# Two up pairs of seven products follow each other, and a down group's first splits stand behind mixer work

## The chip, the cores and the metric

The kernel runs on one core of a Trainium2 chip. The metric is the device time of one execution in microseconds (us), taken as the median of several runs. Engines are named as in the profile: PE (TensorE, matmuls), PEld (TensorE's weight loads), DVE (VectorE), ACT (ScalarE), POOL (GpSimd), SP (SyncE, which only issues transfers).

## The reference, cut to what matters

A trunk of four layers on x of 512 tokens by 1024 channels, all float32. Each layer has a token mixer (convolution, attention on a 64-wide grid, retention, convolution) and then a gated feed-forward part, which is what the change touches:

```
def conv_ffn(h, w_up, dw_w, dw_b, w_down):
    u = dwconv(h @ w_up, dw_w, dw_b)          # 1024 -> 5632 channels, 3 taps over the tokens
    val, gate = jnp.split(u, 2, axis=-1)      # 2816 each
    return (jax.nn.gelu(gate) * val) @ w_down # 2816 -> 1024
...
    h = rmsnorm(x, norm2_g[i])
    x = x + conv_ffn(h, ffn_w_up[i], ffn_dw_w[i], ffn_dw_b[i], ffn_w_down[i])
```

## The kernel before, in words

Channels lie on the 128 partitions and the 512 tokens along the free dimension. A float32 product is made of three passes: each operand is split into a high part (rounded to the matmul's format, a cast on ACT) and a low part (the rest, a subtraction on DVE), and `mm3` (lines 180 to 183) adds high times high, low times high and high times low. So every weight tile that comes in by a transfer costs one ACT cast (line 167) and one DVE subtraction (line 168) in `split_w`. Some up tiles are made in another way (`load_w_acc`, lines 171 to 178): ACT makes both parts and an accumulating transfer on POOL completes the low one.

The feed-forward part (`ffn`, line 298) has 22 pairs j of up tiles, n = 2j (value) and n = 2j + 1 (gate), each of 128 channels by 512 tokens. `ups_of(j)` (line 599) makes pair j, `mids(j)` (line 588) runs the mixer steps up to pair j - 1: the three taps (lines 403 to 407), gelu (411), the product of value and gate (426). Two mixed pairs make one unit H of four quarters and three sums of quarters (lines 426 to 432), which is split into Hh and Hl (line 435, by `split`, lines 191 and 192).

Two places use seven products in place of eight (a 2 by 2 scheme in the manner of Strassen) on matmuls of 256 columns. In the up part, four pairs per layer are made so by `up_macro` (line 373); which ones is in `UPS` (line 78). Its last two products are not made in it but in `finish_up` (line 366), which is called after the next up tile, or inside the next `up_macro`; only then is the sum `s12` (line 371) there for the mixer. In the down part, `down` (line 509) takes four H units as a group and makes four output pairs i = 0 to 3; group 0 starts at pair 8 (in layer 1 at pair 9), group 1 at pair 16 (`starts`, line 612). The first products of i = 0 need only the first three H units of the group, the rest the fourth one too.

The weights for seven products come from `sums` (line 466), transfers only: two loads on SP and one accumulating transfer on POOL into the buffers `ws` (three of them) and `wq` (one), and from `weights` (line 478): one raw load on SP, then six DVE operations and four ACT casts into the buffers wh and wl (three each), h2, l2, h4 and l4 (one each). Raw loads go through two buffers `wr` (line 157). `fetch_sums` (line 595) calls `sums` one pair ahead.

The instructions are not executed in the order of the Python text: a scheduler lays out each engine's queue at compile time. It goes through a simulated time and gives an engine that is free the ready instruction that comes first in the program. So the order of the calls is a priority, and the queues are fixed once they are laid out.

Around the start of a group the text of before is, at lines 613 to 619:

```
for j in range(1, FT):
    ups_of(j)
    w0 = down_w(0, starts[j], state["load"]) if j in starts else None
    if n > S2[l]:
        mids(j)
    if w0:
        down(starts[j], w0, lambda: mids(j + 1), lambda: ups_of(j + 1))
```

Here `down_w` (line 496) is `sums` and `weights` together, so the first weights of a group come before the mixer step of the pair that was made last but one. With `UPS` = (10, 12, 18, 19), and (11, 13, 18, 19) in layer 1, one ordinary pair stands between the first two pairs of seven, and none between the last two.

Of the kernel before, what the change touches and what calls it, by code (L numbers as in the profile page):

```python
# [17 lines left out]
P = 128  # L18
# [56 lines left out]
NT_FFN = 7  # L75
NWS = 3
SCALED = (5, 7, 5, 5)
UPS = ((10, 12, 18, 19), (11, 13, 18, 19), (10, 12, 18, 19), (10, 12, 18, 19))
COMBO = (4, 5, 6, 7)
ACC = tuple(n for n in range(3, 2 * FT, 2) if n // 2 not in (8, 9, 16, 17))  # L80


# [1 line left out]
def tile_trunk(  # L84
# [17 lines left out]
    def nm(s):  # L102
        uid[0] += 1
        return f"{s}{uid[0]}"
# [51 lines left out]
    def load_raw(src, n):  # L156
        raw = wraw.tile([P, D], F32, tag="wr", name=nm("wr"))
        state["load"] = nc.sync.dma_start(raw[:, :n], src)
        return raw
# [4 lines left out]
    def split_w(raw, n, eng):  # L164
        hi = whi.tile([P, D], F32R, tag="wh", name=nm("wh"))
        lo = wlo.tile([P, D], F32R, tag="wl", name=nm("wl"))
        nc.scalar.copy(hi[:, :n], raw[:, :n])  # L167
        eng.tensor_tensor(lo[:, :n], raw[:, :n], hi[:, :n].bitcast(F32), SUB)  # L168
        return hi, lo
# [20 lines left out]
    def split(src, hi, lo, n=None):  # L190
        state["cast"] = nc.scalar.copy(hi, src)  # L191
        return nc.vector.tensor_tensor(lo, src, hi.bitcast(F32), SUB)  # L192
# [38 lines left out]
    state = {"late": [], "squares": []}  # L231
# [66 lines left out]
    def ffn(l, after):  # L298
        with ExitStack() as st:
# [37 lines left out]
            def combos(p):  # L337
                e, o = x[2 * p], x[2 * p + 1]
                c = hp.tile([P, D], F32, tag="ws", name=nm("cx"), bufs=NWS)
                q = [c[:, i * 256:(i + 1) * 256] for i in range(4)]  # L340
                nc.vector.tensor_tensor(q[0], e[:, 256:], e[:, :256], SUB)
                nc.vector.tensor_tensor(q[1], o[:, :256], e[:, :256], SUB)
                nc.vector.scalar_tensor_tensor(q[2], o[:, :256], -1.0, q[0], MUL, SUB)
                nc.vector.scalar_tensor_tensor(q[3], q[2], -1.0, o[:, 256:], MUL, SUB)
                cl[p] = hp.tile([P, D], F32R, tag=f"cl{p}", name=nm("cl"))
                for k, h in ((2 * p, slice(0, T)), (2 * p + 1, slice(T, D))):
                    ch[k] = const.tile([P, T], F32R, tag=f"x{k}", name=nm("ch"))
                    split(c[:, h], ch[k], cl[p][:, h])
# [117 lines left out]
            def sums(src, gate=None):  # L466
                n = src.shape[-1] // 4
                r13 = hp.tile([P, D], F32, tag="ws", name=nm("ws"), bufs=NWS)
                sg = hp.tile([P, D], F32, tag="wq", name=nm("wq"))
                with tc.issue_after(gate.ins) if gate else ExitStack():  # L470
                    nc.sync.dma_start(
                        r13[:, :2 * n].rearrange("p (b n) -> p b n", b=2),
                        src[:, 2 * n:3 * n].unsqueeze(1).broadcast_to([P, 2, n]))
                    nc.gpsimd.dma_start(r13[:, :2 * n], src[:, :2 * n], accum_op=ADD)
                    nc.sync.dma_start(sg[:, n:2 * n], src[:, 3 * n:])
                return src, r13, sg

            def weights(src, r13, sg):
                n = src.shape[-1] // 4
                r1 = load_raw(src[:, :2 * n], 2 * n)  # L480
                w1 = split_w(r1, 2 * n, nc.vector)
                w13 = split_w(r13, 2 * n, nc.vector)
                r2 = r13[:, n:2 * n]
                nc.vector.tensor_tensor(r2, r2, r1[:, :n], ADD)
                h2 = hp.tile([P, T], F32R, tag="h2", name=nm("h2"))
                l2 = hp.tile([P, T], F32R, tag="l2", name=nm("l2"))
                split(r2, h2[:, :n], l2[:, :n])
                nc.vector.tensor_tensor(sg[:, :n], r2, sg[:, n:2 * n], ADD)
                h4 = hp.tile([P, D], F32R, tag="h4", name=nm("h4"))
                l4 = hp.tile([P, D], F32R, tag="l4", name=nm("l4"))  # L490
                split(sg[:, :2 * n], h4[:, :2 * n], l4[:, :2 * n])
                u = lambda w, b: (w[0][:, b * n:(b + 1) * n], w[1][:, b * n:(b + 1) * n])
                return {"a11": u(w1, 0), "a22": u(w1, 1), "s3": u(w13, 0), "s1": u(w13, 1),
                        "s2": u((h2, l2), 0), "sg": u((h4, l4), 0), "a12": u((h4, l4), 1)}

            def down_w(i, q, gate=None):
                p0, p1 = PARTS[q]
                c = PART_COL[q]
                return weights(*sums(f_down[l, i][:, c:c + 4 * (p1 - p0) * P], gate))

            def prod(o, w, q, b, start, stop=True, part=None):
                p0, p1 = PARTS[q]
# [6 lines left out]
            def down(q, first, late, filler):  # L509
                p0, p1 = PARTS[q]  # L510

                def finish(i, w, v, s12):
                    prod(v[:, :256], w["sg"], q, 2, False)
                    prod(v[:, 256:], w["a12"], q, 3, True)
                    nc.vector.tensor_tensor(s12, v, s12, ADD)
                    nc.gpsimd.dma_start(xd[2 * i + 1], s12, accum_op=ADD)

                prev = None
                for i in range(4):
                    w = down_w(i, q) if i else first  # L520
                    xb, v = bank(psa), bank(psa)
                    xc = xb[:, :256]
                    s12 = t512()
                    if i == 0:
                        prod(xc, w["a11"], q, 1, True, part=range(p0, p1 - 1))
                        prod(v[:, 256:], w["a22"], q, 6, True, part=range(p0, p1 - 1))
                    now = range(p1 - 1, p1) if i == 0 else None
                    prod(xc, w["a11"], q, 1, True, part=now)
                    nc.scalar.copy(s12[:, 256:], xc)  # L529
                    prod(v[:, 256:], w["a22"], q, 6, True, part=now)  # L530
                    prod(xc, w["s2"], q, 0, False)
                    nc.scalar.copy(s12[:, :256], xc)
                    prod(v[:, :256], w["s1"], q, 4, True)
                    prod(xc, w["s3"], q, 5, False)
                    u2 = t512()
                    nc.scalar.activation(u2.rearrange("p (h t) -> p h t", h=2),
                                         xc.unsqueeze(1).broadcast_to([P, 2, 256]), AF.Copy, scale=-1.0)
                    nc.vector.tensor_tensor(u2, u2, v, SUB)
                    nc.gpsimd.dma_start(xd[2 * i], u2, accum_op=ADD)
                    if prev:  # L540
                        finish(*prev)
                    prev = (i, w, v, s12)
                late()
                filler()
                finish(*prev)
# [42 lines left out]
            def mids(upto):  # L588
                nonlocal done
                while done < upto:  # L590
                    for _ in mid(done, ups[2 * done], ups[2 * done + 1]):
                        pass
                    done += 1

            def fetch_sums(j):
                if j in UPS[l] and j not in ahead:
                    ahead[j] = sums(f_us[l, UPS[l].index(j)], state["load"])

            def ups_of(j):
                nonlocal n  # L600
                fetch_sums(j + 1)
                if j in UPS[l] and n < 2 * j + 2:
                    ups.extend(up_macro(j))
                    n += 2
                while n < 2 * j + 2:
                    ups.append(up(n))
                    finish_up()
                    n += 1
                if j in COMBO:
                    combos(COMBO.index(j))  # L610

            starts = {2 * p1 + (l == 1 and q == 0): q for q, (_, p1) in enumerate(PARTS)}
            for j in range(1, FT):
                ups_of(j)
                w0 = down_w(0, starts[j], state["load"]) if j in starts else None
                if n > S2[l]:
                    mids(j)
                if w0:
                    down(starts[j], w0, lambda: mids(j + 1), lambda: ups_of(j + 1))
            mids(FT)  # L620
# [684 lines left out]
    kind, l = seq[0]  # L1305
    first = []
# [50 lines left out]
def _layout(inp):  # L1357
# [56 lines left out]
    for sh in range(PH):  # L1414
        for r in range(PH):
# [14 lines left out]
        [fu[l, :, par, :, j + c].transpose(1, 0, 2).reshape(P, T)  # L1430
         for c, par in ((0, 0), (FT, 1), (FT, 0), (0, 1))], -1) for j in UPS[l]]) for l in range(DEPTH)])
    fd = f["ffn_w_down"].reshape(4, FT, P, 8, P)
# [50 lines left out]
```

## Time and profile before

| | |
|---|---|
| median of three runs | 2579.05 us (2576.54 to 2581.14) |
| the profiled execution | 2579.95 us |
| its span, from the first to the last instruction | 2577.9 us |
| granted TensorE clock, mean over the span | 0.993 |

Two lines of the page show how work is spread over the span in 40 equal slices, and how many transfers go with it. Each digit is the busy share of a slice in tenths.

```
PE   9999999999999999899999999999999999999999
DVE  7976867677877776667666565686767887686765
ACT  5555645465556554455332323454545445554543
DMA  6736766743333566574222222567565672477664
```

A row of the groups, the timeline or the waits gives line, engine, operation and the names of the tiles, output before input (wl<-wr,wh is the subtraction that makes a low part). Idle time ahead of an instruction stands in brackets in the timeline, with what ended it. The four feed-forward parts lie in the trace at about 190 to 560 us, 800 to 1190, 1620 to 1990 and 2190 to 2578.

### The profile page before, as it was taken

To read this page: it belongs to the slowest core of one execution; us is meant where nothing else is said; L and a number is where in the kernel's file an instruction comes from. 1 tells how busy PE (TensorE), PEld (TensorE's weight loads), DVE (VectorE), ACT (ScalarE), POOL (GpSimd) and SP (SyncE) were. 2 spreads that over 40 slices of the span, in tenths; PEclk is the share of its full clock that TensorE was granted. 3 is DMA by queue.
4 is the path that set the end of the run, shared out by engine and by line. 5 is a ranking of instruction groups with operands and counts; after the bars stand their busy time and mean duration, and the time that the engine had idled before them with its cause. 6 is when DMAs were issued, how large, how long until landed. Compare 5 with 4: busy or idle time off the path is not lost.

```text
span 2577.9 us, 38787 instructions
## 1 busy us (share of the span) xinstructions
PE 2528.4 (98%) x15166; PEld 2182.9 (85%) x15166; DVE 1826.8 (71%) x3004; ACT 1265.2 (49%) x1763; POOL 387.2 (15%) x476
## 2 busy tenths in 40 slices
PE   9999999999999999899999999999999999999999
PEld 7878897989998888798888888789888888789897
DVE  7976867677877776667666565686767887686765
ACT  5555645465556554455332323454545445554543
POOL 1214010104321211020000000201010121101010
PEclk9999999999999999999999999999999999999999
DMA  6736766743333566574222222567565672477664
GB/s 239 233 100 185 196 156 164 161 142 95 97 91 106 141 179 153 148 185 122 82 75 73 82 77 70 146 170 182 153 151 143 202 228 89 119 190 168 166 152 139
DMA packets 124040, 370.70 MB, mean 144 GB/s; under 512 B 15136, under 2 KB 18080, under 8 KB 123856
## 3 DMA queue, kind: packets, MB, share of 16 engines
q1 hardware_dynamic: 90816, 277.30, 34.2%
q0 software_dynamic: 31744, 88.19, 18.4%
q10 hardware_dynamic: 1296, 2.72, 0.3%
q8 instruction: 119, 1.95, 0.3%
q14 instruction: 65, 0.53, 0.1%
HBM read 333.59 MB, written 30.79 MB: 141 GB/s over the span
## 4 chain that ended last, share of the span: by engine, by line
PE 86%; DVE 6%; DMA 4%; ACT 2%; issue 1%; DVEq 0%; POOL 0%; SPq 0%; ACTq 0%; POOLq 0%
PE ps L182 21%; PE ps L183 21%; PE ps L181 21%; PE ps L316 3%; PE ps L312 3%; PE ps L311 3%; PE ps L187 3%; PE ps L188 3%; PE ps L186 3%; DMA wr<-in_f_down 2%; DVE wl L168 1%; PE ps L743 1%; PE ps L742 1%; PE ps L741 1%; PE ps L454 1%
## 5 line engine op out<-in xcount | busy, mean ns | idle before, releaser
L167 ACT CAST wh<-wr 128x1024 fp32r<-128x1024 f32 (+1 forms) x310 | 317.9, 1027 | 567.9 <-PE ps L182 275.3
L168 DVE TENSOR_TENSOR wl<-wr,wh 128x1024 fp32r<-128x1024 f32 (+1 forms) x307 | 371.0, 1208 | 207.9 <-ACT wh L167 192.5
L182 PE MATMUL ps<-xl,wh 128*128 128x512 f32 (+1 forms) x1248 | 488.2, 391 | 0.0
L181 PE MATMUL ps<-xh,wh 128*128 128x512 f32 (+1 forms) x1248 | 485.9, 390 | 1.4 <-ACT wh L167 1.4
L183 PE MATMUL ps<-xh,wl 128*128 128x512 f32 (+1 forms) x1248 | 484.9, 390 | 0.1
L181 PEld LDWEIGHTS ps<-xh,wh 128*128 128x128 f32 x1248 | 235.1, 188 | 55.3 <-ACT wh L167 2.2
L183 PEld LDWEIGHTS ps<-xh,wl 128*128 128x128 f32 x1248 | 234.8, 188 | 52.6 <-DVE wl L168 0.7
L182 PEld LDWEIGHTS ps<-xl,wh 128*128 128x128 f32 x1248 | 235.1, 188 | 51.9 <-DVE xl L253 0.5
L182 PE MATMUL ps<-Hl,wh 128*128 128x256 f32 (+1 forms) x734 | 228.1, 314 | 6.2 <-DVE Hl L192 6.2
L183 PE MATMUL ps<-Hh,wl 128*128 128x256 f32 (+1 forms) x734 | 225.5, 315 | 7.9 <-DVE wl L168 7.6
L181 PE MATMUL ps<-Hh,wh 128*128 128x256 f32 (+1 forms) x734 | 222.4, 315 | 9.3 <-ACT Hh L191 6.3
L311 PE MATMUL ps<-xh,wh 128*128 128x512 f32 x416 | 164.8, 396 | 1.3 <-ACT wh L175 1.3
L312 PE MATMUL ps<-xl,wh 128*128 128x512 f32 x416 | 164.5, 395 | 0.0
L187 PE MATMUL ps<-wl,xh 128*128 128x256 f32 (+1 forms) x512 | 159.2, 312 | 1.9 <-DVE wl L168 1.9
L186 PE MATMUL ps<-wh,xh 128*128 128x256 f32 (+1 forms) x512 | 159.2, 314 | 1.1 <-ACT xh L250 1.1
L188 PE MATMUL ps<-wh,xl 128*128 128x256 f32 (+1 forms) x512 | 159.3, 312 | 0.0
L181 PEld LDWEIGHTS ps<-Hh,wh 128*128 128x128 f32 x734 | 140.7, 194 | 21.3 <-ACT Hh L191 7.4
L183 PEld LDWEIGHTS ps<-Hh,wl 128*128 128x128 f32 x734 | 142.0, 196 | 17.5 <-DVE wl L168 10.5
L182 PEld LDWEIGHTS ps<-Hl,wh 128*128 128x128 f32 x734 | 142.7, 195 | 15.3 <-DVE Hl L192 7.8
L177 POOL DMA_DIRECT2D wl<-in_f_up x52 | 46.7, 897 | 451.1 <-ACT wl L176 401.9
L316 PE MATMUL ps<-xh,wl 128*128 128x512 f32 x416 | 107.8, 400 | 3.3 <-DMA wl<-in_f_up 3.3
L181 PE MATMUL ps<-Hh,h 128*128 128x256 f32 x384 | 108.9, 284 | 0.5 <-ACT t L529 0.5
(330 smaller groups left out, 6167.9 us busy)
## 6 DMA issues: line engine op xcount, KB each, us to landing
wr<-in_f_up SPq DMA_DIRECT2D x144, 512.0 KB, 4.1
wraw<-in_cdw SPq DMA_DIRECT2D x56, 608.0 KB, 5.2
wl<-in_f_up POOLq DMA_DIRECT2D x52, 512.0 KB, 7.8
ws<-in_f_down SPq DMA_DIRECT2D x32, 512.0 KB, 8.5
wr<-in_f_down SPq DMA_DIRECT2D x32, 512.0 KB, 6.2
ws<-in_f_down POOLq DMA_DIRECT2D x32, 512.0 KB, 8.3
xd<-t POOLq DMA_DIRECT2D x64, 256.0 KB, 6.3
wr<-in_cw_in SPq DMA_DIRECT2D x30, 512.0 KB, 4.1
```

What stands on the lines that cost most here:

```text
L167: nc.scalar.copy(hi[:, :n], raw[:, :n])
L168: eng.tensor_tensor(lo[:, :n], raw[:, :n], hi[:, :n].bitcast(F32), SUB)
L177: nc.gpsimd.dma_start(lo[:, :n], src.bitcast(F32R), accum_op=ADD)
L181: nc.tensor.matmul(o, wh, ah, start=first, stop=False, skip_group_check=free)
L182: nc.tensor.matmul(o, wh, al, start=False, stop=False, skip_group_check=free)
L183: nc.tensor.matmul(o, wl, ah, start=False, stop=last, skip_group_check=free)
L186: nc.tensor.matmul(o, ah, wh, start=first, stop=False)
L187: nc.tensor.matmul(o, ah, wl, start=False, stop=False)
L188: nc.tensor.matmul(o, al, wh, start=False, stop=last)
L311: nc.tensor.matmul(ps, wh[:, s], xhi[k], start=k == 0, stop=False)
L312: nc.tensor.matmul(ps, wh[:, s], xlo[k], start=False, stop=False)
L316: nc.tensor.matmul(ps, wl[:, k * P:(k + 1) * P], xhi[k], start=False, stop=k == KD - 1)
```

## The change

In layers 0, 2 and 3 the second pair of seven products moves from 12 to 11, in layer 1 from 13 to 12, so that it follows the first one directly; the arrays of weight sums are laid out to match. And `down_w` becomes `down_sums`, the transfers alone; `weights`, with the raw load, the casts and the subtractions of the group's first output pair, is called behind `mids(j)`. The new loop over `COMBO` makes the same calls as the old lookup.

```
-UPS = ((10, 12, 18, 19), (11, 13, 18, 19), (10, 12, 18, 19), (10, 12, 18, 19))
-COMBO = (4, 5, 6, 7)
+UPS = ((10, 11, 18, 19), (11, 12, 18, 19), (10, 11, 18, 19), (10, 11, 18, 19))
+COMBO = (4,5,6,7)
+LATEW = True
...
-            def down_w(i, q, gate=None):
+            def down_sums(i, q, gate=None):
                 p0, p1 = PARTS[q]
                 c = PART_COL[q]
-                return weights(*sums(f_down[l, i][:, c:c + 4 * (p1 - p0) * P], gate))
+                return sums(f_down[l, i][:, c:c + 4 * (p1 - p0) * P], gate)
...
-                    w = down_w(i, q) if i else first
+                    w = weights(*down_sums(i, q)) if i else first
...
-                if j in COMBO:
-                    combos(COMBO.index(j))
+                for p in range(4):
+                    if COMBO[p] == j:
+                        combos(p)
...
-                w0 = down_w(0, starts[j], state["load"]) if j in starts else None
+                w0 = down_sums(0, starts[j], state["load"]) if j in starts else None
+                if w0 and not LATEW:
+                    w0 = weights(*w0)
                 if n > S2[l]:
                     mids(j)
+                if w0 and LATEW:
+                    w0 = weights(*w0)
                 if w0:
                     down(starts[j], w0, lambda: mids(j + 1), lambda: ups_of(j + 1))
```

## The prediction

> **What bounds the kernel now.** I read the page's head first, to see which engine has no slack.
>
> ```profile
> span 2577.9 us, 38787 instructions
> PE 2528.4 (98%) x15166; PEld 2182.9 (85%) x15166; DVE 1826.8 (71%) x3004; ACT 1265.2 (49%) x1763; POOL 387.2 (15%) x476
> ```
>
> TensorE is busy 98% of the span, and the change neither adds nor removes a matmul. So time can only come from TensorE's idle stretches, and from stretches in which its clock is low. The view of waits, for TensorE alone, names the idle ones.
>
> ```profile
> PE ps L183 <- DVE wl L168: 7.6, 3, 2.9
> PE ps L181 <- ACT Hh L191: 6.3, 3, 2.9
> PE ps L182 <- DVE Hl L192: 6.2, 7, 1.3
> PE ps L181 <- ACT wh L167: 4.2, 6, 1.3
> PE ps L316 <- DMA wl<-in_f_up: 3.3, 1, 3.3
> ```
>
> The first four rows are waits of the kind that the start of a down group can have: for split weights (wh, wl) and for the split mixer output (Hh, Hl). I looked for their places, which are the first products of the eight down groups (two in each layer), and asked the view by stretches for each. Columns: length, busy time of TensorE, matmuls (the count also holds one to three that only cross an edge), granted clock, DMA share, GB/s.
>
> ```profile
> core 0: us, PE busy (x), PEclk, DMA share, GB/s
> 328.31:334.01 5.70, 5.70 (x51) 1.00 0.97 179
> 309.00:314.25 5.25, 5.03 (x41) 1.00 0.56 192
> 942.31:950.46 8.15, 7.38 (x61) 1.00 0.57 164
> 1741.34:1747.32 5.98, 5.04 (x42) 1.00 0.58 183
> 2309.93:2316.19 6.26, 5.00 (x41) 1.00 0.54 173
> 436.65:457.93 21.28, 16.76 (x123) 0.92 0.47 120
> 1065.67:1092.89 27.22, 20.30 (x124) 0.81 0.40 107
> 1869.70:1892.48 22.78, 17.47 (x123) 0.93 0.49 127
> 2438.59:2461.25 22.66, 18.98 (x123) 0.77 0.49 128
> 986.52:999.72 13.20, 9.86 (x39) 0.74 0.82 171
> ```
>
> The first row is undisturbed: 48 matmuls of 256 columns begin in 5.70 us, 0.1188 us each. The next four are the starts of the first groups (40, 60, 40 and 40 matmuls begin): they should take 4.75, 7.12, 4.75 and 4.75, so they lose 0.5, 1.0, 1.2 and 1.5, **4.2 us together**. The four after them are the starts of the second groups, 122 matmuls each, which should take 14.5: they lose 6.8, 12.7, 8.3 and 8.2, **36.0 us together**. Idle time explains only part: length less busy time is 4.5, 6.9, 5.3 and 3.7, in sum 20.4. The other 15.6 us are matmuls at the lower granted clock (0.92, 0.81, 0.93, 0.77) that follows the idle time. The Trainium skill (TensorE: Matmul & The Clock Gate, Why this matters for your kernels) asks for idle gaps over about 3 us before the clock drops; here none in these groups is over 2.9 us (the waits above) and it drops all the same, so the measurement decides. By that page the groups would be worth their 20.4 us of idle alone, and the sum below would give about 2566 us.
>
> **Why the second group's start is late.** Two things in the trace. First, the chain of the two products-of-seven before it ends late. Its beginning is the first copy out of the first pair (ACT L379), its end the last sum of the second pair (DVE L371); the mixer work of that pair and, in the order of the queues, of the pairs behind it waits for this sum.
>
> ```profile
> 362.82 0.36 ACT L379 COPY t<-ps 128x256 f32<-128x256 f32 x1
> 410.71 0.69 DVE L371 TENSOR_TENSOR t<-ps,t 128x512 f32<-128x512 f32 x1 [0.22 <-PE ps L183]
> 999.92 0.37 ACT L379 COPY t<-ps 128x256 f32<-128x256 f32 x1 [8.28 <-PE ps L183]
> 1049.51 0.68 DVE L371 TENSOR_TENSOR t<-ps,t 128x512 f32<-128x512 f32 x1
> 496.87 0.36 ACT L379 COPY t<-ps 128x256 f32<-128x256 f32 x1
> 529.46 0.69 DVE L371 TENSOR_TENSOR t<-ps,t 128x512 f32<-128x512 f32 x1 [2.04 <-PE ps L183]
> ```
>
> Layer 0's pairs 10 and 12 take 47.9 us from the one to the other, layer 1's pairs 11 and 13 take 49.6. Then the second group begins 25.9 us later in layer 0 (436.65), 16.2 us later in layer 1 (1065.67). The shorter lead has the larger loss: 12.7 against 6.8 (8.3 and 8.2 in layers 2 and 3, where pairs 10 and 12 stand as in layer 0; mean 7.8). Pairs 18 and 19, which already follow each other, take 32.6 us.
>
> Second, the group's own first splits stand in VectorE's queue ahead of mixer work. This is layer 2.
>
> ```profile
> 1864.24 1.05 ACT L167 CAST wh<-wr 128x1024 fp32r<-128x1024 f32 x1 [4.76 <-DMA wr<-in_f_down]
> 1865.33 1.23 DVE L168 TENSOR_TENSOR wl<-wr,wh 128x1024 fp32r<-128x1024 f32 x1 [3.96 <-ACT wh L167]
> 1867.80 1.22 DVE L168 TENSOR_TENSOR wl<-ws,wh 128x1024 fp32r<-128x1024 f32 x1
> 1869.05 0.69 DVE L484 TENSOR_TENSOR ws<-ws,wr 128x512 f32<-128x512 f32 x1
> 1869.78 0.69 DVE L488 TENSOR_TENSOR wq<-ws,wq 128x512 f32<-128x512 f32 x1
> 1872.32 0.68 DVE L192 TENSOR_TENSOR l<-ws,h 128x512 fp32r<-128x512 f32 x1
> 1872.93 1.22 DVE L192 TENSOR_TENSOR l<-wq,h 128x1024 fp32r<-128x1024 f32 x1
> 1879.76 2.02 DVE L192 TENSOR_TENSOR Hl<-F,Hh 128x1792 fp32r<-128x1792 f32 x1 [1.76 <-ACT Hh L191]
> ```
>
> The weights' lower half waits 3.96 us for a cast that waits for its transfer, and everything behind it on VectorE waits too. With the 5.7 us of the six splits and sums (1.23 + 1.22 + 0.69 + 0.69 + 0.68 + 1.22) that is 9.7 us ahead of the last mixer split, Hl, which ends at 1881.8, 12 us after TensorE reached the group.
>
> **The change, part by part.**
>
> *What is added and removed:* nothing. Each layer keeps four products-of-seven, the same count of split and of accumulating loads, and the same products; the loop over COMBO that replaces a lookup does the same.
>
> *The second pair moves up by one.* Price on TensorE: the pairs that already follow each other show it.
>
> ```profile
> 486.00:531.00 45.00, 45.00 (x291) 1.00 0.74 185
> 1121.00:1166.00 45.00, 45.00 (x292) 1.00 0.74 188
> 1921.00:1966.00 45.00, 45.00 (x289) 1.00 0.73 184
> 2489.00:2535.00 46.00, 46.00 (x297) 1.00 0.74 180
> ```
>
> TensorE has no idle time in them, at full clock: while the second pair waits for its single-buffered sums (wq, h4, l4), matmuls of the following up pairs fill in. I take zero. If that cover is missing, the price is that of the one place where a transfer was late among such pairs, 986.52 to 999.72: 22 matmuls of 512 columns and 14 of 256 are 58 times 0.1188, 6.9 us of work, so 6.3 are lost, and 25.2 if each layer paid it. Its cause is in the next two rows: on POOL's queue a sum for a pair of seven waits for its first transfer, and an up tile's accumulating transfer stands behind it.
>
> ```profile
> 982.07 0.89 POOL L474 DMA_DIRECT2D ws<-in_f_us  x1 [4.83 <-DMA ws<-in_f_us]
> 983.16 1.60 POOL L177 DMA_DIRECT2D wl<-in_f_up  x1
> ```
>
> The moved pair brings with it two loads on SP and one such accumulating transfer on POOL, ahead of the loads of one ordinary up pair (two on SP, one accumulating on POOL). On SP its wq load waits until the first pair's sums are split, and raw loads of up tiles stand behind it. Behind 18 and 19 the same order stands and costs nothing, so I keep zero; layer 1's own 6.3 us lie before its moved pair, and I leave them in.
>
> *What the earlier chain gives.* If 10 and 11 take the 32.6 us of 18 and 19, the last sum is 15.3 us earlier in layers 0, 2 and 3 (lead 41.2 in place of 25.9) and 17.0 in layer 1 (lead 33.2 in place of 16.2). Between the leads 16.2 and 25.9 the loss falls from 12.7 to 7.8, 0.51 us for each us of lead. Carried on, that is 4.1 at 33.2 and zero at 41.2; below the level of the first groups, which have no such pair before them, I do not go: 4.2 / 4 = 1.05. What is left is 4.1 + 3 x 1.05 = 7.2 us of 36.0, so **28.8 us gained**. Bounds: nothing (0) to all of it (36.0). What is late next at a second group is the raw load of its first weights.
>
> *The splits behind the mixer work.* Per group six VectorE operations and four ScalarE casts change places with one mixer step; the load of the raw weights moves past it too, but a mixer step issues nothing on SP. At the first groups the most to gain is their 4.2 us. The most to lose: the cast and the lower half (1.05 + 1.23 = 2.3 us, layer 2's rows) come after the last Hl instead of beside it, four times 9.2 less the 4.2 already paid, 5.0. I take zero there; at the second groups it helps the same stall that is already counted.
>
> *Sum.* The profiled execution took 2579.95 us (span 2577.9 and 2.05 around it), 0.9 above the median of the runs, 2579.05. 2579.95 - 28.8 = 2551.2; on the median's footing 2550.3. I say 2551.
>
> **The rivals.** A difference under about 0.2% (5 us) can't be told from no change here.
>
> *Half of it (2567).* The order in the queues is laid out at compile time from modelled durations, and the 3.96 us wait for the raw weights stays ahead of mixer work. For: SP issues that load only when a raw buffer comes free, which the change does not touch. Against: the mixers' backlog ahead is gone by then. Then each second group keeps its wait, about 4 us and a short stretch of low clock, 6 us x 4 = 24 left, 12 gained.
>
> *No difference (2579).* The last mixer step, pair 15, may be bound by its own chain from the up pair that ends 11 us before the group. Against: in the first groups the same chain ends in time.
>
> *Slower (2600).* VectorE and ScalarE take their queues in order, as the 3.96 us show. Put behind the mixer step, the group's first weights may come after TensorE has reached the group, at all eight groups. In layer 2, 9.7 us less work ahead of it lets Hl end at 1872.1; cast and lower half follow until 1874.4, 4.7 us after TensorE came at 1869.70, plus 1.7 for one low stretch at about half speed. At the first groups that is 4 x 6.4 - 4.2 = 21 more, and at the second nothing less if the earlier sum buys nothing. It decides from 3.3 us of lateness: 3.3 + 1.7 = 5.0, the mean of the eight losses today. Against: today the lower half is there at 1866.6, 3.1 us early. The Trainium skill (TensorE: Matmul & The Clock Gate, Architectural detail) calls the queues of ScalarE and VectorE strictly first in, first out, which is the rule that speaks against this half of the change; the trace agrees.
>
> *All of it (2539).* Both kinds of groups lose nothing: 40.2 us.
>
> **How the numbers follow.** The forecast, 2541 to 2562, has 0.63; half of it 0.16; all of it 0.06; no difference 0.06; slower 0.09. The first three are faster: 0.85. The range of 8 in 10 takes the forecast and half of it with a margin: 2541 to 2569.
>
> **What would show it.** Right: the stretches at the starts of the second groups at 15 to 19 us for 122 matmuls with the clock at 1.00; L379 to the second L371 about 33 us; the waits on Hh, Hl and wl together under 8 us where they are 20 now; TensorE still without idle time through pairs 10 and 11. Wrong: TensorE's waits on wh or wl at the first product of a group over 3 us; a wait on an accumulating up transfer after pair 11; or the second groups' loss unchanged with the last sum 15 us earlier, which would make the lead the wrong cause.

## The result, and the profile after

The changed kernel takes 2547.36 us (median of five runs, 2545.83 to 2551.38) against 2579.05: the ratio is 0.988, with a 95% interval of 0.9865 to 0.9894, 31.7 us less. The forecast was 2551, and the range 2541 to 2569.

The head of the page of the profiled execution (2551.38 us):

```profile
span 2549.5 us, 38773 instructions
PE 2516.3 (99%) x15166; PEld 2174.0 (85%) x15166; DVE 1831.9 (72%) x3004; ACT 1266.3 (50%) x1763; POOL 387.1 (15%) x476
```

The same matmuls, 28.4 us less span. The starts of the groups of the changed kernel, 122 matmuls in each row, first and second group of layers 0 to 3 in turn (length, busy time of TensorE, matmuls, clock, DMA share, GB/s; undisturbed, 122 matmuls take 14.5 us):

```profile
core 0: us, PE busy (x), PEclk, DMA share, GB/s
310.35:325.35 15.00, 14.80 (x124) 1.00 0.67 189
438.01:454.53 16.52, 15.02 (x123) 1.00 0.64 176
940.17:955.71 15.54, 14.77 (x123) 1.00 0.66 178
1065.11:1080.60 15.49, 14.77 (x123) 1.00 0.66 188
1728.91:1744.66 15.75, 14.79 (x124) 1.00 0.66 184
1857.32:1872.86 15.54, 14.75 (x124) 1.00 0.67 187
2289.95:2304.49 14.54, 14.54 (x124) 1.00 0.62 176
2417.15:2432.81 15.66, 14.76 (x124) 1.00 0.67 186
```

The second groups lose 2.0, 1.0, 1.0 and 1.2 us, 5.2 together where it was 36.0: **30.8 us come from there**, and the clock stays at 1.00 in all of them. The first groups lose 0.5, 1.0, 1.2 and 0.0, 1.4 us less than before. Together that is some 32 us, more than the 28.4 by which the profiled span shrank: this execution, the slowest of the five, has two stretches of 3.4 us at a granted clock of 0.50, from 134.8 and from 585.3 us on, where the profiled execution of before stays at 1.00, and they cost 3.4 us.

In the view of waits for TensorE, Hh and Hl have left the head of the list (12.5 us before; the groups' waits on Hh, Hl and wl together are 0.8 us where they were 20):

```profile
PE ps L182 <- ACT wh L168: 5.6, 8, 1.4
PE ps L317 <- DMA wl<-in_f_up: 4.6, 1, 4.6
```

The chain of the first two pairs of seven in layer 0, from the first copy to the last sum (lines are one or more further on than before):

```profile
364.17 0.36 ACT L380 COPY t<-ps 128x256 f32<-128x256 f32 x1
396.67 0.69 DVE L372 TENSOR_TENSOR t<-ps,t 128x512 f32<-128x512 f32 x1 [3.15 <-PE ps L184]
```

That is 32.5 us where it was 47.9. Layer 2's second group starts at 1857.32; these are rows of its first weights and of the last mixer steps ahead of it (others stand between them):

```profile
1847.97 1.05 ACT L168 CAST wh<-wr 128x1024 fp32r<-128x1024 f32 x1 [3.11 <-DMA wr<-in_f_down]
1849.06 1.22 DVE L169 TENSOR_TENSOR wl<-wr,wh 128x1024 fp32r<-128x1024 f32 x1 [2.14 <-ACT wh L168]
1850.20 0.74 DVE L406 SCALAR_TENSOR_TENSOR t<-ps,par,t 128x511 f32<-128x511 f32 x1
1851.46 0.74 DVE L408 SCALAR_TENSOR_TENSOR t<-ps,par,t 128x511 f32<-128x511 f32 x1
1852.96 0.69 DVE L427 TENSOR_TENSOR F<-t,t 128x512 f32<-128x512 f32 x1 [0.76 <-ACT t L412]
1853.69 0.69 DVE L430 TENSOR_TENSOR F<-F 128x512 f32<-128x512 f32 x1
1855.43 0.42 DVE L432 SCALAR_TENSOR_TENSOR F<-F 128x256 f32<-128x256 f32 x1
1856.37 0.42 DVE L433 SCALAR_TENSOR_TENSOR F<-F 128x256 f32<-128x256 f32 x1
1858.73 2.02 DVE L193 TENSOR_TENSOR Hl<-F,Hh 128x1792 fp32r<-128x1792 f32 x1 [0.74 <-ACT Hh L192]
```

Hl ends 3.4 us after TensorE reached the group; it was 12.1. And the group's first low half still stands ahead of the mixer operations, with a wait of 2.14 us. So the half of the change that was to put it behind them has not done so here.

### The profile page after: what moved, and what is told of

Same layout as the page of the kernel before. It is cut to its first block, busy times and chain, and to the rows that moved or that the text cites. A ratio compares the mean times of both kernels' runs of the same rounds, so it can differ in the third digit from the quotient of the medians.

```text
span 2549.5 us, 38773 instructions
## 1 busy us (share of the span) xinstructions
PE 2516.3 (99%) x15166; PEld 2174.0 (85%) x15166; DVE 1831.9 (72%) x3004; ACT 1266.3 (50%) x1763; POOL 387.1 (15%) x476
## 4 chain that ended last, share of the span: by engine, by line
PE 86%; DVE 5%; DMA 4%; ACT 3%; issue 2%; DVEq 0%; ACTq 0%; POOL 0%; SPq 0%; POOLq 0%
PE ps L182 21%; PE ps L183 21%; PE ps L184 21%; PE ps L317 3%; PE ps L313 3%; PE ps L312 3%; PE ps L188 3%; PE ps L187 3%; PE ps L189 3%; DMA wr<-in_f_down 3%; DVE wl L169 1%; PE ps L749 1%; PE ps L748 1%; PE ps L747 1%; ACT wh L168 1%
## 5 line engine op out<-in xcount | busy, mean ns | idle before, releaser
L183 PE MATMUL ps<-Hl,wh 128*128 128x256 f32 (+1 forms) x734 | 222.3, 307 | 0.8 <-DVE Hl L193 0.8
L182 PEld LDWEIGHTS ps<-Hh,wh 128*128 128x128 f32 x734 | 136.9, 188 | 16.2 <-ACT wh L168 8.7
```

The lines of the kernel that those rows point to most:

```text
L182: nc.tensor.matmul(o, wh, ah, start=first, stop=False, skip_group_check=free)
L183: nc.tensor.matmul(o, wh, al, start=False, stop=False, skip_group_check=free)
```

## The experiments

The measure in all of them is the loss at the starts of the four second groups: length of the stretch with the first 122 matmuls, less 14.5 us. The lead is the time from the start of the last sum of the first two pairs of seven to the start of that group. Lead and loss are read from one profiled execution of each kernel. Times are medians; ratios are to the kernel before, measured on the same chip.

| kernel | time | ratio (95%) | lead, layers 0 to 3 | loss, layers 0 to 3 |
|---|---|---|---|---|
| before | 2579.05 | | 25.9, 16.2, 25.9, 25.9 | 6.8, 12.7, 8.3, 8.2 |
| changed | 2547.36 | 0.988 (0.9865 to 0.9894) | 41.3, 33.6, 41.3, 41.3 | 2.0, 1.0, 1.0, 1.2 |
| e1 pairs alone | 2549.18 | 0.9881 (0.9868 to 0.9895) | 41.3, 33.6, 41.3, 41.3 | 3.5, 1.3, 1.5, 1.0 |
| e2 splits alone | 2579.06 | 0.9998 (0.9988 to 1.0007) | 25.9, 16.2, 25.9, 25.9 | 6.9, 14.6, 10.8, 7.4 |
| e3 next to each other, late | 2571.54 | 0.9966 (0.9953 to 0.9978) | 19.9, 7.7, 19.9, 19.9 | 8.0, 9.9, 6.6, 8.9 |
| e4 changed, tile 21 split | 2547.05 | 0.9865 (0.985 to 0.9881) | 41.3, 30.4, 41.3, 41.3 | 2.2, 2.7, 1.1, 1.4 |
| e5 splits forced behind | 2593.33 | 1.0052 (1.0036 to 1.0068) | 29.2, 16.3, 29.2, 29.2 | 9.4, 14.4, 10.0, 8.4 |
| e6 before, three raw buffers | 2574.04 | 0.9974 (0.9965 to 0.9984) | 30.5, 14.7, 25.9, 27.3 | 7.8, 11.9, 7.9, 6.8 |
| e7 four placings | 2564.43 (one run) | | 16.1, 19.9, 31.3, 16.6 | 10.5, 5.4, 0.8, 7.7 |
| e8 changed, more VectorE work | 2578.21 | 0.9997 (0.9987 to 1.0006) | 41.3, 33.6, 41.3, 41.3 | 9.9, 9.5, 8.9, 9.4 |
| e9 spread, group later | 2575.13 (one run) | | 37.1, 27.1, 37.1, 37.1 | 0, 1.0, 0, 0 |
| e10 before, less VectorE work | 2554.92 | 0.9908 (0.9893 to 0.9923) | 28.0, 18.2, 28.0, 28.0 | 1.0, 10.7, 1.0, 1.0 |
| e11 changed, three raw buffers | 2537.64 | 0.9841 (0.9826 to 0.9856) | 41.1, 33.6, 41.3, 41.3 | 0, 0, 0, 0 |
| e12 as e11, tile 21 split | 2539.62 | 0.985 (0.9834 to 0.9867) | 41.4, 34.7, 41.3, 41.3 | 0, 0.2, 0, 0 |

**Which half of the change does it: e1 and e2.**

```
e1:  -LATEW = True
     +LATEW = False
e2:  -UPS = ((10, 11, 18, 19), (11, 12, 18, 19), (10, 11, 18, 19), (10, 11, 18, 19))
     +UPS = ((10, 12, 18, 19), (11, 13, 18, 19), (10, 12, 18, 19), (10, 12, 18, 19))
```

> The changed kernel with the group's first splits ahead of the mixer step as before; only the second pair of seven has moved up. Theory of the lead (what counts is how long before the second group the last sum of the pairs of seven ends, since mixer work queues behind it): the lead is as in the changed kernel, so nearly all of the gain stays, 2547 to 2553 us, and the second groups lose together at most 8 us of the 36 before. Theory of the queue (what counts is that the group's first splits, with their wait for a transfer, stand ahead of mixer work on VectorE): half or more of the loss comes back, 2562 to 2579 us, with a wait of 3 to 4 us before a wl ahead of the last mixer operations.

> The kernel before with only the group's first splits put behind the mixer step; the pairs of seven stay at 10 and 12, 11 and 13. Theory of the lead: the last sum stays 26 and 16 us ahead of the second group, the backlog of mixer work stays, and at most the 9.7 us of splits and wait go from ahead of Hl: 2565 to 2580 us. Theory of the queue: Hl comes some 9 us earlier and the second groups lose at most 10 us together: 2548 to 2556 us.

The second groups of e1:

```profile
439.63:457.66 18.03, 16.52 (x123) 0.91 0.58 161
1065.04:1080.88 15.84, 14.78 (x123) 1.00 0.63 184
1857.45:1873.48 16.03, 14.74 (x123) 1.00 0.64 181
2416.49:2432.03 15.54, 14.75 (x124) 1.00 0.64 187
```

The pairs alone bring the whole gain, the splits alone nothing that can be measured. Layer 2 of e2 shows why:

```profile
1866.57 1.23 DVE L169 TENSOR_TENSOR wl<-wr,wh 128x1024 fp32r<-128x1024 f32 x1 [3.96 <-ACT wh L168]
1880.99 2.02 DVE L193 TENSOR_TENSOR Hl<-F,Hh 128x1792 fp32r<-128x1792 f32 x1 [1.75 <-ACT Hh L192]
```

The first low half waits 3.96 us, 14.4 us ahead of Hl, as before the change (3.96 and 14.4), and the operations between them are the same. The place of the call is only a priority, and the queue is laid out as it was. That holds for the whole trace: buffer numbers left aside, every engine executes the same instructions in the same order in e2 as in the kernel before (all 3004 of VectorE, all 15166 matmuls), and in e1 as in the changed kernel. Moving the call changed nothing in the order of what ran.

So these two pairs also show what chance does to one order of instructions: layer 2's second group loses 8.3 us in the one execution and 10.8 in the other, layer 0's 2.0 and 3.5. Differences of up to 2.5 us in the loss of one group say nothing by themselves.

**What if the splits really stand behind: e5.** An ordering edge on VectorE, from the group's last mixer split to the first weights' operations there, with the pairs at their old places.

```
-                split(F, hi, lo)
+                state["H"] = split(F, hi, lo)
...
                 if w0 and LATEW:
-                    w0 = weights(*w0)
+                    with behind("H"):
+                        w0 = weights(*w0)
```

> Pairs of seven as in the kernel before (10 and 12; 11 and 13). In e2 the call was moved but VectorE's queue at the second groups stayed as it was, the group's first wl with its 4 us wait ahead of the last mixer operations; here an ordering edge forces the DVE part of the first splits behind the last mixer split Hl of the group. Theory of the queue, now really tried: Hl comes up to 9.7 us earlier at the second groups, which lose 10 to 20 us together in place of 36: 2555 to 2570 us. Rival (the slower case of the prediction): TensorE reaches the group before the first low half is there, at all eight groups: 2590 to 2605 us, with waits on wl of 3 to 5 us at the first products of the first groups too.

TensorE's waits in e5, and ScalarE's cast of a raw weight ahead of layer 2's second group:

```profile
PE ps L182 <- ACT wh L168: 19.7, 10, 5.8
PE ps L184 <- DVE wl L169: 16.2, 11, 8.3
1875.14 1.05 ACT L168 CAST wh<-wr 128x1024 fp32r<-128x1024 f32 x1 [8.59 <-DMA wr<-in_f_down]
```

It is slower by 0.5%. At the second groups TensorE waits 2.9 to 5.8 us for wh and in layer 1 another 8.3 for wl, in the way of the rival that I had put at 2600 us, and the loss there is 42.2 us, 6 more than before. At the first groups the rival did not come: no such wait is over 0.8 us, where it had 3 to 5, and they lose 7.1 us together in place of 4.2. The casts on ScalarE were not moved, and one of them waits 8.6 us for its transfer ahead of mixer work. A clean order of both engines was not tried.

**Following each other, or the lead: e3, e7 and e9.** Splits ahead as before in all three.

```
e3:  +UPS = ((12, 13, 18, 19), (13, 14, 18, 19), (12, 13, 18, 19), (12, 13, 18, 19))
e7:  +UPS = ((11, 13, 18, 19), (12, 13, 18, 19), (11, 12, 18, 19), (10, 13, 18, 19))
e9:  +UPS = ((10, 12, 19, 20), (11, 13, 19, 20), (10, 12, 19, 20), (10, 12, 19, 20))
     -            starts = {2 * p1 + (l == 1 and q == 0): q ...
     +            starts = {2 * p1 + (l == 1 or q == 1): q ...
```

> Splits ahead of the mixer step as before; the first two pairs of seven follow each other, but late: 12 and 13, and 13 and 14 in layer 1. Two more ordinary pairs (22.4 us) come first, so the last sum is at 362.8 + 22.4 + 32.6 = 418 us in layer 0, a lead of 19 us, and 11 us in layer 1. Theory of the lead: by 0.51 us of loss for each us of lead the second groups lose 3 x 11.4 + 15.5 = 50 us together, 14 more than the kernel before: 2593 us. Theory that following each other is itself the cause (the ordinary pair between them stretches the chain): the gain stays, 2550 to 2556 us.

> One kernel, four placings, splits ahead of the mixer step as before; read from the starts of the second groups by layer (122 matmuls, 14.5 us undisturbed). Layer 0: 11 and 13, spread and late. Layer 1: 12 and 13, following each other. Layer 2: 11 and 12, following each other. Layer 3: 10 and 13, spread wide. By the lead with the mixer steps that are left to do in it: losses of about 12, 8, 1 to 2 and 10 to 13 us. If following each other is what counts: 8, 1, 1 and 8 or more.

> Pairs 10 and 12 (11 and 13) as before, spread, splits ahead of the mixer step; but the second group begins one pair later, at pair 17, with the same H units, and the last two pairs of seven move to 19 and 20 to make room. So the last sum keeps its place and the lead grows by 11.2 us, to 37 us in layers 0, 2 and 3 and 27 us in layer 1. Theory of VectorE's backlog ahead of the group: losses at the second groups of about 1 us in layers 0, 2 and 3 and up to 5 in layer 1. Theory that the two pairs have to follow each other: the losses stay at 7 to 8 and 12 us. The total time isn't compared, since the end of the layer is laid out anew.

The second groups of e3, of e7 and of e9:

```profile
436.38:458.85 22.47, 17.82 (x123) 0.85 0.45 125
1061.93:1086.32 24.39, 17.92 (x124) 0.86 0.43 119
1862.62:1883.75 21.13, 16.78 (x123) 0.92 0.47 120
2429.85:2453.23 23.38, 19.06 (x124) 0.78 0.46 123
```

```profile
437.60:462.61 25.01, 18.04 (x123) 0.86 0.43 116
1067.81:1087.66 19.85, 15.28 (x124) 1.00 0.48 132
1864.32:1879.58 15.26, 14.78 (x123) 1.00 0.63 187
2423.48:2445.72 22.24, 17.05 (x123) 0.92 0.43 115
```

```profile
449.40:463.88 14.48, 14.48 (x123) 1.00 0.61 181
1079.42:1094.95 15.53, 14.76 (x123) 1.00 0.66 180
1880.13:1894.62 14.49, 14.49 (x124) 1.00 0.62 181
2447.70:2462.18 14.48, 14.48 (x123) 1.00 0.62 181
```

Following each other is neither enough (e3, and e7's layer 1: losses of 5.4 to 9.9) nor needed (e9: pairs 10 and 12, losses of 0). In e7 the losses stand in the order that was expected by the lead, and are smaller (10.5, 5.4, 0.8 and 7.7). But the lead alone isn't the rule either: e3's layer 1 has the shortest lead of all, 7.7 us, and loses 9.9, less than the 12.7 of the kernel before at 16.2. Both theories of e3 missed its time.

e9 frees the starts of the second groups, but not the kernel: its one run takes 2575.13 us, about as long as before. TensorE's waits in it lie elsewhere, none of these at the start of a second group:

```profile
PE ps L317 <- DMA wl<-in_f_up: 15.3, 5, 4.2
PE ps L182 <- ACT Hh L192: 7.2, 4, 1.8
```

**What has to be done within the lead: e8 and e10.** VectorE's work for each ordinary pair, from the rows of layer 2 above: four operations on the taps (4 x 0.74), the product (0.69), half of a unit's sums and split (0.69 + 0.42 + 0.42 + 2.02, halved: 1.8) and the low half of the one up tile that is not accumulated (1.22), in sum 6.7 us; and once the group's own first splits, 5.7.

```
e8:                          pass
     +                    if done in (12, 13, 14):
     +                        scr = hp.tile([P, T], F32, tag="scr", name=nm("scr"))
     +                        with behind("mid"):
     +                            for _ in range(8):
     +                                nc.vector.tensor_tensor(scr, rstd_bc, rstd_bc, ADD)
                           done += 1
e10: -                acc = n in ACC
     +                acc = n in ACC or n in (26, 28, 30)      # pairs at 10 and 12 as before
```

> The changed kernel with extra work on VectorE that nothing uses: after the mixer steps of pairs 12, 13 and 14 eight additions of 128 by 512 each, 24 x 0.685 = 16.4 us per layer, about the 15.3 us by which the last sum has come forward. If the backlog on VectorE ahead of the group is the cause, the loss of the second groups comes back with it: 25 to 40 us together, 2570 to 2585 us. If it is the order or the latency of the chain of sums that counts, the groups lose a few us only: 2547 to 2555 us.

> The kernel before, splits ahead of the mixer step, with less work on VectorE ahead of the second group: up tiles 26, 28 and 30 get their low half by an accumulating transfer, 1.24 us each off VectorE and about as much onto ScalarE, 3.7 us in layers 0, 2 and 3 and 2.5 in layer 1. Theory of the backlog: the second groups lose about 3 to 4 us less each, 22 to 26 together, 2565 to 2570 us. Rival (the transfers, at 0.8 of the DMA engines' time in that stretch, are no quicker): waits on wl from in_f_up take their place, 2577 to 2590 us.

The second groups of e8 and of e10:

```profile
435.55:459.98 24.43, 18.14 (x123) 0.79 0.44 119
1067.25:1091.23 23.98, 17.62 (x123) 0.86 0.44 120
1866.70:1890.09 23.39, 17.50 (x123) 0.85 0.47 124
2436.02:2459.89 23.87, 17.68 (x124) 0.86 0.45 122
```

```profile
435.83:451.36 15.53, 14.76 (x124) 1.00 0.64 176
1059.75:1084.91 25.16, 20.39 (x124) 0.73 0.43 116
1861.59:1877.12 15.53, 14.77 (x124) 1.00 0.63 178
2421.21:2436.73 15.52, 14.75 (x124) 1.00 0.63 177
```

With the lead untouched, the additions take the whole gain back (loss 37.7 in place of 5.2). Not all of the 16.4 us count: of the 24 additions in a layer, 19 run before the last Hl (15 in layer 1), which is 13.0 us (10.3). And with the pairs where they were, e10 loses 1.0 us in place of about 8 at three of the four groups; layer 1, with the shortest lead and only two tiles moved, keeps its 10.7. Its time is 10 us below the range of its theory. e10 is the less clean of the two: besides the 3.7 us of work, its lead is 2.1 us longer, and layer 2's first wl waits 1.2 us in place of 4.0. **So VectorE's work ahead of the group is shown by e8 to be enough to bring the loss back, and e10 agrees.**

A balance, drawn up after the runs, puts most cases in order: the lead, less 6.7 us for each pair from the last pair of seven to pair 15, less 5.7. Before: 25.9 - 32.5 = -6.6, and 16.2 - 25.8 = -9.6 in layer 1. Changed: 41.3 - 39.2 = +2.1 and +1.1. e9: +4.6 and +1.3. e7: -9.7, -5.9, -1.2, -9.2. e10: -0.8 and -5.1 in layer 1. Every group at -1.2 or above loses at most 2.0 us (e1's layer 0: 3.5), every one at -5.1 or below at least 5.4. In between it doesn't tell: e4's layer 1, at -2.1, loses 2.7, and e6's layer 0, at -2.0, loses 7.8; e5, with another order, is left aside. Beyond that the size is rough: e3's layer 1, at -11.4, loses 9.9, and e8, at about -11 and -9, loses 9 to 10. The balance counts work alone. In the leads of the kernel before, VectorE is busy for 23.6, 11.9, 21.4 and 22.4 us, and the rest are waits for ScalarE, so a queue that holds waits is part of the backlog.

**What is left: e4, e6, e11 and e12.** Three raw buffers (e6 on the kernel before, e11 on the changed one); in layer 1, tile 21 split in place of accumulated (e4); both on the changed one (e12).

```
e6, e11, e12:  -NRAW = 2
               +NRAW = 3
e4, e12:       -                acc = n in ACC
               +                acc = n in ACC and not (l == 1 and n == 21)
```

> The changed kernel; one more thing: in layer 1 up tile 21 is split by ScalarE and VectorE like the others beside a group, in place of the accumulating transfer for which TensorE waits 4.6 us there (and then has 6.8 us at the low clock). If POOL's order of transfers is the cause of that wait: 7 to 8 us less than the changed kernel, about 2540 us. If VectorE is too full there (1.24 us more work) and the wait only changes its name to wl: no difference, 2545 to 2550 us.

> The kernel before with three raw buffers in place of two, so that the raw load of the group's first weights is issued without waiting for the up tiles' splits. If the wait for that transfer (3.0 to 4.0 us on VectorE in layers 1 to 3) is what makes the second groups late: they lose about 3.5 us less each, 2563 to 2568 us. If the backlog of mixer work is: the idle time on VectorE goes but the end of the mixer chain hardly moves, 2574 to 2580 us.

> The changed kernel with three raw buffers in place of two. In the kernel before they gave 5.6 us, though its second groups lost as much as with two. If the gain has nothing to do with the second groups, it comes here too: 2540 to 2544 us. If it was the backlog's wait for the transfer after all, nothing is left to gain: 2546 to 2549 us.

> The changed kernel with three raw buffers and with layer 1's up tile 21 split by ScalarE and VectorE in place of the accumulating transfer. If both small gains add to that of the change: 2536 to 2541 us. If what they free is taken back at the next group's start (as tile 21's in e4): 2545 to 2549 us.

The second groups of e11:

```profile
435.88:450.41 14.53, 14.53 (x123) 1.00 0.60 174
1054.08:1068.61 14.53, 14.53 (x123) 1.00 0.62 173
1844.48:1858.97 14.49, 14.49 (x123) 1.00 0.61 173
2403.74:2418.23 14.49, 14.49 (x123) 1.00 0.62 172
```

On the kernel before, the third buffer hardly helps the second groups: 34.4 us lost in place of 36.0, with TensorE idle for 19.0 of them in place of 20.4, although layer 2's first wl no longer waits for its raw load. So that wait alone was not their cause. The profile of e6 is that of the slowest of its ten executions (2578.78 us), so it doesn't show where the 5.6 us of the median come from, nor whether the second groups have a part in them.

On the changed kernel the backlog is gone and that wait is what ends last; without it no second group loses anything, and e11, at 2537.64 us, is the fastest of all, ratio 0.9841 against the 0.988 of the changed kernel, below both of its ranges. Of the 9.7 us between the two, 5.2 are those of the second groups; where the rest comes from was not taken apart (the mean clock is 0.999 in the one profile and 0.997 in the other). e4 takes away layer 1's wait for the accumulating transfer, and the time is 2547.05, not 2540. That is in the range of its second theory, but no wait on wl has come in its place. In its profile layer 1's second group loses 2.7 and layer 3's first 3.9 us, 1.7 and 3.8 more than in the changed kernel; whether the tile's split causes this or chance is open. e12, 2539.62 (0.985, 0.9834 to 0.9867), can't be told from e11.

## Why the prediction was right

- *Where the time would come from:* the second groups, 28.8 us forecast, 30.8 measured, with the low clock gone as well as the idle time. Right. One reading in it was off: of the 36.0 us, 15.6 were put down to the low clock, but the clocks of the same rows (0.08, 0.19, 0.07 and 0.23 missing over 21.28, 27.22, 22.78 and 22.66 us) make 13.7; the other 1.9 stay unexplained.
- *The chain of 32.6 us in place of 47.9, as 18 and 19 show it:* 32.5. Right.
- *Following each other costs TensorE nothing at pairs 10 and 11:* in layers 0, 2 and 3 the waits show nothing there; layer 1 has one of 0.2 us. Right.
- *Layer 1's wait for an accumulating transfer stays:* 3.3 us before, 4.6 now. Right.
- *0.51 us of loss for each us of lead, read from two points:* this was the right sign with the wrong quantity. The work that VectorE has to do within the lead counts as much as its length (e8, e10), and past the balance the loss falls to about 1 us rather than along a line: layer 1 was to keep 4.1 us and kept 1.0. That the sum came out near was in this part luck: every second group of the changed kernel happens to be on the good side, and the floor of 1.05 us, taken from the first groups, was close to what is left there.
- *The splits' wait as the second cause, and the splits behind the mixer step as its remedy:* this step failed. The call's place moved no operation at all (the order of e2 is that of the kernel before), e1 has the gain without it, and the wait by itself was nearly without effect at the second groups while the backlog lasted (e6). It is the next thing to go after the backlog (e11). The sum had added nothing for it, so the forecast did not suffer.
- *Half of it:* the condition of this rival came true, the wait for the raw weights stayed ahead of mixer work (2.14 us in layer 2). Its price did not: with the backlog gone a second group keeps 1.0 to 2.0 us, not 6, as the rival's own "against" had it.
- *The slower case:* it did not come with the change, but forced behind (e5) the splits make the kernel slower, 2593 us, with TensorE waiting for wh and wl at the second groups, and hardly at the first.
- *By the Trainium skill (TensorE: Matmul & The Clock Gate, Why this matters for your kernels), which asks for no idle gaps over about 3 us, the gain would have been an estimated 13 us, the 20.4 of idle time less the 7.2 left:* it was 31.7. In the kernel before, the low clock came at groups where no wait is over 2.9 us, and it is gone with these waits.

## What to carry to other kernels

Where a group of products needs the outputs of another engine, count that engine's work from the last event that holds it up to the group's start, and compare it with the time there is: here the loss set in when the work no longer fitted, and it cost the low clock on top of the idle time. Moving the event earlier or some work to another engine helped the whole kernel; moving the group later freed its start and moved the waits elsewhere (e9). Where a scheduler lays out the queues, compare the order of the instructions in the two traces before anything is put down to a moved call: here the order was the same, and half of the change was no change.

## What the runs showed of the hardware

The same idle time can cost clock or not: the kernel before has waits of 1.9, 1.3 and 1.3 us at layer 0's second group and a clock of 0.92 there; e7 has waits of 1.9, 1.3 and 1.3 at layer 1's and the clock stays at 1.00 (19.85 us against 21.28 for the same matmuls). Behind layer 0's feed-forward part both kernels have waits of 1.1 and, 11 us later, 1.8 to 1.9 us: at 575 and 586 us before, where the clock stays at 1.00, and at 572 and 583 us in the changed kernel, where 3.4 us at 0.50 follow. And in e11 a single wait of 3.2 us, in layer 1 at 981 us, is followed by no low clock.

The low stretches in the traces are 3.4 us or a multiple of it (3.4, 6.8, 10.2, and 13.7 in e5 and e10), at half the clock, so each step of 3.4 costs 1.7 us. What decides whether idle time brings one, its sum over some time or where it falls, no run here separates.
